# A hybrid decoder layer: merge gates in a stage of their own by seven block products in place of eight, sums moved between VectorE, GpSimd and ScalarE

## The chip, the cores and the metric

The kernel runs on one core of one Trainium2 chip. Five engines take part: TensorE (PE, with its weight loads PEld) multiplies, VectorE (DVE), ScalarE (ACT) and GpSimd (POOL) work on elements, and SyncE (SP) issues most of the DMA transfers; GpSimd issues some. The metric is the device time of one execution in microseconds, the median over runs. A profiled execution gives the trace from which all rows below come.

## What is computed

A decoder layer on 2048 tokens of width 1024, in float32. Of the reference this matters:

```python
h = einsum('bsd,dn->bsn', x, w_in) + b_in      # x: 2048 x 1024
c_q, c_kv, k_pe, z_a, u, v, z_b, g_a, g_b = split_columns(h)
#  384,  128,   32, 512, 512, 512, 512, 1024, 1024 columns
y_a = mla_attention(c_q, c_kv, k_pe, ...) * silu(z_a)   # 8 heads, causal
y_b = spatial_gating(u, v, ...) * silu(z_b)
merged = sigmoid(g_a) * (y_a @ w_oa) + sigmoid(g_b) * (y_b @ w_ob)
out = layer_norm(alpha * x + merged @ w_out)
```

The columns z_a, u, z_b, g_a and g_b are called features here; g_a and g_b are the two merge gates.

## The kernel before

**Precision.** Every float32 factor is cut into a high and a low part. `split` (L65 to L67) does it with a ScalarE cast (high) and a VectorE subtraction (low, L67). `mm3` (L69) then multiplies three times: high by high, high by low, low by high. One such step is three matmuls, nearly always with a 128x128 weight and 512 columns.

**Stages.** x is read in four chunks c of 512 tokens, kept as xh and xl, two chunks at a time. Up to 178.2 us the latents are projected and raised to queries, keys and values. Up to 319.3 the spatial gating unit (SGU) computes v, normalises and mixes it (`mix`), turns the result by `ptu` transposes, and stores it as mo to mxd (L481, L482). Then attention runs with the features as fill, and from 1405.6 on the last stage forms the gated outputs, their product with w_ab, the product with w_out, and the layer norm.

**Features.** There are 28 tiles of 128 columns: ZA, U, ZB with 4 each, GA, GB with 8 each (MT_ORDER is their order). `gates()` is a generator. `weights(m)` loads a tile's weights (fst) and splits them (fwh, fwl, L66 and L67). `group(m, c)` does eight steps into one PSUM tile psg and yields after each. A gate then needs one ScalarE tanh (L525) and a store to gd from GpSimd (L526); the other features pass through `finish` with VectorE operations on ft, fo and gu. Each tile's weights are loaded twice, for chunks 0 and 1 and then for 2 and 3.

**Attention.** Blocks of one head h and one chunk c follow each other, 32 in all. For a block, `top` multiplies queries by keys into pss and VectorE takes row maxima mx (L639); after the last, dg, a diagonal of negated maxima, is built on VectorE (L644) and `shift` turns it into an extra row of Q. `score(k)` multiplies a block of 128 keys, on partitions, by 512 queries (three matmuls into pst); ScalarE takes the exponential p and casts ph, VectorE subtracts pl (L67), and GpSimd adds p to acc (L675). `product` multiplies ph and pl by V into po. Behind the last k, acc is split into ah and al, and `total` sums it over keys. p, ph and pl have three buffers each, pst two in PSUM, Q three.

**Order.** TensorE keeps the order in which the program is written (`keep`). Products lag scores by two steps, tops run up to LEAD = 6 steps ahead by a list of due times. Each call of `work(cost)` adds to a credit, and whenever that reaches half a fill step, one step of `gates()` is put in; `rate` is chosen so that 36 steps are left for the end. 48 steps stand ahead of attention and 12 more near its start. On the other engines a scheduler sets the order; `high_priority` moves work forward.

## Time and profile before

| | us |
|---|---|
| median of three runs (1777.47 to 1780.12) | 1778.77 |
| the profiled execution, its time | 1779.64 |
| the profiled execution, span from first to last instruction | 1777.9 |
| attention with its 48 fills ahead and 36 behind | 319.3 to 1405.6 |

A share is an engine's busy time over the span. A stretch's row tells how long each engine was busy in it and with how many instructions (a few matmul records are missing), and then the clock granted to TensorE as a part of full speed. In a timeline row the bracket tells how long the engine was idle before the instruction and what ended that. Matmuls overlap in the trace, so their rate is read from a stretch and not from one's length.

### The profile page before, as it was taken

What the parts mean: (1) busy time and instruction counts of PE and PEld (TensorE: products, weight loads), DVE (VectorE), ACT (ScalarE), POOL (GpSimd) and SP (SyncE); (2) the same over time, 40 slices, a digit from 0 to 9 for tenths busy, and PEclk for the clock granted to TensorE, in tenths of its full rate; (3) what the DMA queues carried; (4) which work ended last, traced back from release to release, by engine and by line L of the source; (5) the groups of instructions that cost most, each with busy time, mean ns of one, the idle gap of its engine ahead of it and who ended that gap; (6) DMA issues with size and microseconds to landing.
All of it is one profiled execution on the core that took longest, in us unless ns stands there. A gap on an engine that the chain in (4) does not pass through costs nothing.

```text
span 1777.9 us, 23031 instructions
## 1 busy us (share of the span) xinstructions
PE 1712.2 (96%) x8064; PEld 1422.2 (80%) x8064; DVE 1274.9 (72%) x2241; ACT 804.9 (45%) x1468; POOL 471.6 (27%) x520
## 2 busy tenths in 40 slices
PE   8999999999999999999899999899999899999998
PEld 8899877778888778888688887788888678888886
DVE  7855686378877777667788878676766568777664
ACT  6533442245565545456566565455556331303020
POOL 0000011023444334444344444244444000000000
PEclk9999999999999999999899999899999999999999
DMA  6754841721132242142531222421120888667341
GB/s 211 228 194 157 269 158 48 173 94 57 60 113 78 70 140 67 60 128 92 154 111 54 76 83 74 119 84 66 60 77 30 267 281 268 215 197 217 121 130 71
DMA packets 105092, 229.19 MB, mean 129 GB/s; under 512 B 11720, under 2 KB 28360, under 8 KB 103952
## 3 DMA queue, kind: packets, MB, share of 16 engines
q1 hardware_dynamic: 94480, 194.16, 34.8%
q0 software_dynamic: 10496, 33.56, 5.5%
q8 instruction: 63, 1.03, 0.2%
q14 instruction: 53, 0.43, 0.1%
HBM read 155.70 MB, written 71.97 MB: 128 GB/s over the span
## 4 chain that ended last, share of the span: by engine, by line
PE 62%; DVE 7%; ACT 4%; issue 4%; DMA 2%; POOL 0%; SPq 0%; DVEq 0%; ACTq 0%; POOLq 0%
PE psg L87 25%; PE po L87 16%; PE pst L87 9%; PE pb L87 5%; PE pa L87 4%; PE pss L87 3%; DVE pl L67 2%; DVE mx L639 1%; ACT p L669 1%; DMA Q<-qrd 1%; ACT ph L66 1%; DVE fwl L67 1%; DMA wabst<-in_w_ab_dram 1%; PE pbl L87 1%; DVE dg L644 0%
## 5 line engine op out<-in xcount | busy, mean ns | idle before, releaser
L67 DVE TENSOR_TENSOR pl<-p,ph 128x512 fp32r<-128x512 f32 (+1 forms) x320 | 308.9, 966 | 191.7 <-ACT ph L66 182.2
L675 POOL TENSOR_TENSOR acc<-acc,p 128x512 f32<-128x512 f32 (+3 forms) x288 | 333.5, 1158 | 415.9 <-ACT p L669 414.4
L87 PE MATMUL psg<-xh,fwh 128*128 128x512 f32 x896 | 357.9, 399 | 0.0
L87 PE MATMUL psg<-xl,fwh 128*128 128x512 f32 x896 | 355.8, 397 | 0.0
L87 PE MATMUL psg<-xh,fwl 128*128 128x512 f32 x896 | 354.9, 396 | 0.0
L669 ACT ACTIVATE p<-pst 128x512 f32<-128x512 f32 (+1 forms) x320 | 170.7, 534 | 376.4 <-DVE pst L668 174.6
L87 PE MATMUL pst<-Q,K 97*128 97x512 f32 (+3 forms) x960 | 249.4, 368 | 0.0
L87 PEld LDWEIGHTS pst<-Q,K 96*128 96x128 f32 (+1 forms) x960 | 177.0, 192 | 32.9
L639 DVE TENSOR_REDUCE mx<-pss 128x1 f32<-128x512 f32 (+3 forms) x320 | 190.8, 602 | 17.3 <-PE pss L87 13.4
L87 PEld LDWEIGHTS psg<-xh,fwl 128*128 128x128 f32 x896 | 170.9, 191 | 38.1
L87 PEld LDWEIGHTS psg<-xl,fwh 128*128 128x128 f32 x896 | 172.1, 192 | 31.7
L87 PEld LDWEIGHTS psg<-xh,fwh 128*128 128x128 f32 x896 | 171.7, 192 | 31.8
L66 ACT CAST ph<-p 128x512 fp32r<-128x512 f32 (+1 forms) x320 | 178.1, 557 | 9.1
L87 PE MATMUL pss<-K,Q 96*128 96x512 f32 (+2 forms) x320 | 118.1, 382 | 25.5 <-DMA Q<-qrd 17.0
L78 POOL TENSOR_TENSOR rs<-tm,half 128x1 f32<-128x1 f32 x32 | 24.7, 770 | 421.9 <-DVE tm L77 421.9
L87 PE MATMUL po<-ph,V 128*128 128x512 f32 (+1 forms) x320 | 117.0, 366 | 5.4 <-DVE o L694 5.4
L87 PE MATMUL po<-pl,V 128*128 128x512 f32 (+1 forms) x320 | 117.1, 366 | 0.0
L67 DVE TENSOR_TENSOR fwl<-fst,fwh 128x512 fp32r<-128x512 f32 x112 | 88.9, 800 | 23.0 <-ACT fwh L66 22.9
L87 PE MATMUL po<-woh,mh 128*128 128x512 f32 x256 | 100.6, 394 | 0.0
L87 PE MATMUL po<-woh,ml 128*128 128x512 f32 x256 | 99.7, 391 | 0.0
L87 PE MATMUL po<-wol,mh 128*128 128x512 f32 x256 | 99.5, 389 | 0.0
L87 PEld LDWEIGHTS pss<-K,Q 96*128 96x128 f32 x320 | 61.6, 194 | 43.9 <-DVE mx L639 11.0
(219 smaller groups left out, 3092.8 us busy)
## 6 DMA issues: line engine op xcount, KB each, us to landing
fst<-in_w_feat_dram SPq DMA_DIRECT2D x56, 512.0 KB
gd<-fo POOLq DMA_DIRECT2D x96, 256.0 KB, 2.3
wabst<-in_w_ab_dram SPq DMA_DIRECT2D x32, 512.0 KB
xst<-in_xT_dram SPq DMA_DIRECT2D x31, 512.0 KB
kd<-e SPq DMA_DIRECT2D x16, 512.0 KB
vd<-ve SPq DMA_DIRECT2D x16, 512.0 KB
qnd<-e SPq DMA_DIRECT2D x16, 512.0 KB
V<-vd SPq DMA_DIRECT2D x8, 1024.0 KB
```

The source lines that it names most:

```text
L66: act.copy(hi, src)
L67: dve.tensor_tensor(lo, src, hi.bitcast(F32), op=ALU.subtract)
L78: pool.tensor_tensor(dst, tmp, half, op=ALU.pow)
L87: inorder(pe.matmul(*args, **kw))
L639: dve.tensor_reduce(self.mx[:, j, i:i + 1], ps[:, :n], axis=AX.X, op=ALU.max)
L669: act.activation(p[:, q0:], ps[:, q0:], AF.Exp)
L675: pool.tensor_tensor(self.acc[:, q0:], self.acc[:, q0:], p[:, q0:], op=ALU.add)
```

## The change

It has five parts.

1. **Gates.** MT_ORDER loses GA and GB, which leaves 12 feature tiles as fill, 1152 matmuls in place of 2688. A new stage between the SGU and attention computes the gates in 16 quads. A quad is the 2x2 block product of two weight tiles (GA+m, GB+m; their two halves of 512 rows are w11, w21 and w12, w22) with two chunks of x (their halves). It takes seven products (A, B, C, D, E, where A and D take two each) of 4 steps, in place of eight, from sums of blocks (Strassen's method in Winograd's form). Per quad four combinations of weights and seven low parts are GpSimd tensor_tensor operations, seven high parts are ScalarE casts, and VectorE does five additions out of PSUM. Sums of x are made on VectorE once per two chunks, for quads 0 and 8. Results pass through a tanh on ScalarE and a GpSimd store, as before.
2. **fwl** (weights of the remaining features) and **al** go from VectorE to GpSimd.
3. **dg** goes from one VectorE operation to four ScalarE activations of 128x128.
4. **Q** has four buffers, gu two in place of three.
5. The fill takes chunks 2 and 3 first, then 0 and 1, which are loaded again; 45 steps are left for the end. x is kept in halves (`x_half`, `xk`). The last `mix` is put under `high_priority`.

The core of the diff (the sums s3, s2 and s4 are built as s1 is):

```diff
-MT_ORDER = [m for f in range(4) for m in (MT_U + f, MT_ZB + f, MT_ZA + f)] + list(range(MT_GA, MT))
+MT_ORDER = [m for f in range(4) for m in (MT_U + f, MT_ZB + f, MT_ZA + f)]
...
-        mix(*pend)
+        with tc.high_priority():
+            mix(*pend)
+    with ExitStack() as ph:
...
+        def sums(c0, c1, have):
...
+            if not have:
+                halves(a, *xt[c0][0])
+            yield xt[c0][0]
+            if not have:
+                halves(c, *xt[c1][1])
+            yield xt[c1][1]
+            if not have:
+                raw(c0, 1, d)
+                halves(d, *xt[c0][1])
+            yield xt[c0][1]
+            combine(d, b, c, ALU.add)
+            s = new(1)
+            halves(d, *s)
+            yield s
...
+        def columns(m1, m2):
...
+            def cut(v):
+                hi = dw.tile([P, 4, P], F32R, tag="wh", name="dwh")
+                lo = dw.tile([P, 4, P], F32R, tag="wl", name="dwl")
+                act.copy(hi, v)
+                pool.tensor_tensor(lo, v, hi.bitcast(F32), op=ALU.subtract)
+                return hi, lo
+            pool.tensor_tensor(t1, w12, w11, op=ALU.subtract)
+            pool.tensor_tensor(t2, w22, t1, op=ALU.subtract)
+            pool.tensor_tensor(t4, w21, t2, op=ALU.subtract)
+            pool.tensor_tensor(w12, w22, w12, op=ALU.subtract)
+            for v in (w11, t4, w21, t1, w12, t2, w22):
+                yield cut(v)
+        def product(ps, w, x, more=False):
+            for j in range(4):
+                for i, (a, b) in enumerate(((0, 0), (0, 1), (1, 0))):
+                    mm(ps, w[a][:, j, :], x[b][:, j, :], start=not more and j == 0 and i == 0,
...
+        def out_of(src, c, m, add=None):
...
+                dve.tensor_tensor(o, src, add, op=ALU.add)
+                act.activation(o, o, AF.Tanh, scale=0.5, bias=bfh[:, m:m + 1])
+            pool.dma_start(gd[c][m], o)
...
+                if i == 0:
+                    act.copy(self.u2, self.A)
+                elif i == 2:
+                    out_of(self.A, self.c0, self.m1)
+                elif i == 5:
+                    dve.tensor_tensor(self.u2, self.B, self.u2, op=ALU.add)
+                    dve.tensor_tensor(u3, self.C, self.u2, op=ALU.add)
+                    out_of(self.D, self.c1, self.m2, u3)
+                    out_of(self.E, self.c1, self.m1, u3)
+                elif i == 6:
+                    out_of(self.D, self.c0, self.m2, self.u2)
...
+            for i in range(1, NPROD):
+                if i == NPROD - 1 and nx:
+                    nx.run(0)
+                q.run(i)
+                follow()
...
-                split(st[:, k:k + 4, :], wh[:, k:k + 4, :], wl[:, k:k + 4, :])
+                act.copy(wh[:, k:k + 4, :], st[:, k:k + 4, :])
+                pool.tensor_tensor(wl[:, k:k + 4, :], st[:, k:k + 4, :], wh[:, k:k + 4, :].bitcast(F32),
...
-        for cs2 in ((0, 1), (2, 3)):
+        for cs2 in ((2, 3), (0, 1)):
...
-                self.Qt = kp.tile([DH + 1, 2, C], F32R, tag="Q", bufs=3, name="Q")
+                self.Qt = kp.tile([DH + 1, 2, C], F32R, tag="Q", bufs=4, name="Q")
...
-                        dve.tensor_tensor(self.dg, ident.unsqueeze(1).to_broadcast([P, 4, P]),
-                                          nm.to_broadcast([P, 4, P]), op=ALU.mult)
+                        for e in range(4):
+                            act.activation(self.dg[:, e, :], ident, AF.Copy, scale=nm[:, e, :])
...
-                        split(self.acc, self.ah, self.al)
+                        act.copy(self.ah, self.acc)
+                        pool.tensor_tensor(self.al, self.acc, self.ah.bitcast(F32), op=ALU.subtract)
...
-        rate = (len(MT_ORDER) * 4 * 8 - 48 - 12 - 36) * STEP_NS / (cols * MM_NS)
+        rate = (len(MT_ORDER) * 4 * 8 - 48 - 12 - 45) * STEP_NS / (cols * MM_NS)
```

Three places show what is moved. The first is TensorE in the middle of attention; psg is the fill, pst the scores, po the products, pss the tops; a number in a name is that of a buffer. Before, in a row:

```order
L87 MATMUL psg<-xh_8595,fwh 128x512
L87 MATMUL psg<-xl_8596,fwh 128x512
L87 MATMUL psg<-xh_8595,fwl 128x512
L87 MATMUL psg<-xh_8351,fwh 128x512
L87 MATMUL psg<-xl_8352,fwh 128x512
L87 MATMUL psg<-xh_8351,fwl 128x512
L87 MATMUL po<-ph,V 128x512
L87 MATMUL po<-pl,V 128x512
L87 MATMUL psg<-xh_8351,fwh 128x512
L87 MATMUL psg<-xl_8352,fwh 128x512
L87 MATMUL psg<-xh_8351,fwl 128x512
L87 MATMUL pss<-K,Q 128x512
```

and after the change:

```order
L87 MATMUL psg<-x_2950,fwh 128x512
L87 MATMUL psg<-x_2951,fwh 128x512
L87 MATMUL psg<-x_2950,fwl 128x512
L87 MATMUL pst<-Q,K 128x512 x3
L87 MATMUL po<-ph,V 128x512
L87 MATMUL po<-pl,V 128x512
L87 MATMUL pss<-K,Q 128x512
L87 MATMUL psg<-x_2950,fwh 128x512
L87 MATMUL psg<-x_2951,fwh 128x512
L87 MATMUL psg<-x_2950,fwl 128x512
L87 MATMUL pst<-Q,K 128x512 x3
```

A score, its product and a top now follow each other with one step of fill or none between, where two or three stood.

The second is TensorE at the end of the SGU stage. Before, the last transposes and then the first fill:

```order
L479 MATMUL ptu<-ident,um 128x128 [waits Activation_49]
L479 MATMUL ptu<-ident,um 128x128 x3
L87 MATMUL psg<-xh_2948,fwh 128x512
L87 MATMUL psg<-xl_2949,fwh 128x512
L87 MATMUL psg<-xh_2948,fwl 128x512
```

after the change, the same transposes and then the new stage, with what its first matmul waits for (DMASW are the queues of GpSimd's stores):

```order
L477 MATMUL ptu<-ident,um 128x128 [waits Activation_49]
L477 MATMUL ptu<-ident,um 128x128 x3
L87 MATMUL dA<-x_2950,dwh 128x512 [waits DMASW3_49,DMASW4_49,DMASW2_49,DMASW5_49,DMASW1_49,DMASW6_49,DMASW0_49,DMASW7_49,PE_49,Activation_49]
L87 MATMUL dA<-x_2951,dwh 128x512
L87 MATMUL dA<-x_2950,dwl 128x512 [waits Pool_49]
```

The first matmul of the new stage waits for all of GpSimd's stores, where that of the fill waited for none of them.

The third is VectorE behind the SGU stage. Before, features of the first fills (ft, gu, fo) and their weights:

```order
L541 TENSOR_SCALAR ft<-ft 128x512
L542 TENSOR_TENSOR ft<-ft,fo 128x512
L546 SCALAR_TENSOR_TENSOR gu<-ft,fo 128x512
L67 TENSOR_TENSOR fwl<-fst,fwh 128x512 x2
L541 TENSOR_SCALAR ft<-ft 128x512
L542 TENSOR_TENSOR ft<-ft,fo 128x512
L546 SCALAR_TENSOR_TENSOR gu<-ft,fo 128x512
L552 SCALAR_TENSOR_TENSOR fo<-ft,fo 128x512
L554 TENSOR_TENSOR fo<-fo,gu 128x512
L67 TENSOR_TENSOR fwl<-fst,fwh 128x512 x2
```

after the change, between quad 6's last output (do) and quad 7's additions (du, from PSUM tiles dp); x, xsum and s are parts and sums of x for quad 8:

```order
L601 TENSOR_TENSOR do<-dD,du_4551 128x512
L67 TENSOR_TENSOR x_2981<-xraw,x_2980 128x512 x4
L67 TENSOR_TENSOR x_2953<-xsum_3563,x_2952 128x512 x3
L533 TENSOR_TENSOR xsum_3563<-xsum_3562,xraw 128x512 x2
L67 TENSOR_TENSOR x_2953<-xsum_3563,x_2952 128x512
L533 TENSOR_TENSOR xsum_3563<-xsum_3562,xraw 128x512 x2
L67 TENSOR_TENSOR s_4828<-xsum_3563,s_4827 128x512 x4
L533 TENSOR_TENSOR xsum_3562<-xraw,xsum_3562 128x512 x4
L67 TENSOR_TENSOR s_4859<-xsum_3562,s_4858 128x512 x4
L637 TENSOR_TENSOR du_4699<-dp,du_4699 128x512
L533 TENSOR_TENSOR xsum_3563<-xsum_3563,xraw 128x512
L639 TENSOR_TENSOR du_4882<-dp,du_4699 128x512
```

Twenty-four operations on x stand between the two now, in a stage whose outputs go through VectorE.

## Rows read from the trace of the kernel before

**Rows 1.** the page: busy time of each engine, and the stores of features from GpSimd.

```profile
PE 1712.2 (96%) x8064; PEld 1422.2 (80%) x8064; DVE 1274.9 (72%) x2241; ACT 804.9 (45%) x1468; POOL 471.6 (27%) x520
gd<-fo POOLq DMA_DIRECT2D x96, 256.0 KB, 2.3
```

**Rows 2.** stretches from 319.3 on: length, then busy us of each engine (x instructions).

```profile
core 0: us, PE busy (x) PEld busy (x) DVE busy (x) ACT busy (x) POOL busy (x), PEclk, DMA share, GB/s
319.30:352.50 33.20, 33.20 (x146) 27.54 (x145) 9.92 (x17) 10.90 (x18) 3.03 (x6) 0.98 0.87 203
352.50:1378.80 1026.30, 995.40 (x4449) 820.07 (x4447) 773.37 (x1239) 570.84 (x1044) 419.38 (x439) 0.98 0.27 86
1378.80:1405.60 26.80, 26.27 (x117) 21.23 (x115) 13.32 (x21) 9.53 (x16) 2.75 (x5) 1.00 0.79 245
1405.60:1777.90 372.30, 355.43 (x1536) 289.56 (x1536) 259.92 (x394) 76.67 (x98) 15.38 (x17) 0.99 0.59 193
```

**Rows 3.** the same middle stretch, instructions that touch fwl alone.

```profile
352.50:1378.80 1026.30, 322.08 (x812) 154.78 (x811) 82.11 (x102) 0.98 0.27 86
```

**Rows 4.** what TensorE and its weight load waited for, 319.3 to 1405.6: us, times, longest.

```profile
PE pss L87 <- DMA Q<-qrd: 17.0, 5, 4.9
PEld pss L87 <- DVE mx L639: 11.0, 15, 2.6
PEld pss L87 <- DVE al L67: 10.2, 3, 3.4
```

**Rows 5.** short stretches, same columns as Rows 2.

```profile
390.00:400.00 10.00, 10.00 (x45) 8.16 (x44) 9.87 (x17) 6.88 (x12) 5.18 (x5) 1.00 0.27 78
900.00:950.00 50.00, 49.98 (x225) 40.84 (x224) 43.64 (x69) 30.06 (x54) 22.12 (x20) 1.00 0.21 70
1417.00:1423.00 6.00, 6.00 (x14) 4.26 (x15) 3.15 (x5) 1.67 (x2) 0.00 (x0) 0.50 0.95 321
1600.00:1650.00 50.00, 50.00 (x221) 41.30 (x221) 37.41 (x52) 16.98 (x22) 0.00 (x0) 1.00 0.70 217
```

**Rows 6.** VectorE's groups in 352.5 to 1378.8: busy us, mean ns of one.

```profile
L67 DVE TENSOR_TENSOR pl<-p,ph 128x512 fp32r<-128x512 f32 (+1 forms) x320 | 308.9, 966 | 191.7 <-ACT ph L66 182.2 <-PE psg L87 6.8 <-PE pss L87 0.9
L639 DVE TENSOR_REDUCE mx<-pss 128x1 f32<-128x512 f32 (+3 forms) x320 | 190.8, 602 | 17.3 <-PE pss L87 13.4
L67 DVE TENSOR_TENSOR fwl<-fst,fwh 128x512 fp32r<-128x512 f32 x102 | 82.1, 811 | 16.1 <-ACT fwh L66 15.9
L644 DVE TENSOR_TENSOR dg<-ident,nm 128x512 fp32r<-128x512 f32 x32 | 30.6, 956 | 0.7
L67 DVE TENSOR_TENSOR al<-acc,ah 128x512 fp32r<-128x512 f32 x31 | 21.4, 691 | 6.4 <-ACT ah L66 6.0
```

**Rows 7.** GpSimd's groups, shapes kept apart, same columns.

```profile
L675 POOL TENSOR_TENSOR acc<-acc,p 128x512 f32<-128x512 f32 x192 | 260.4, 1356 | 266.8 <-ACT p L669 265.5
L526 POOL DMA_DIRECT2D gd<-fo x64 | 36.2, 565 | 74.7 <-ACT fo L525 70.5 <-issue 3.6
```

**Rows 8.** timeline (start, length in us): acc and pl together, and pl alone.

```profile
611.50 0.69 DVE L67 TENSOR_TENSOR pl<-p,ph 128x512 fp32r<-128x512 f32 x1 [1.31 <-ACT ph L66]
...
728.96 1.29 POOL L675 TENSOR_TENSOR acc<-acc,p 128x512 f32<-128x512 f32 x1 [1.05 <-ACT p L669]
729.49 1.31 DVE L67 TENSOR_TENSOR pl<-p,ph 128x512 fp32r<-128x512 f32 x1 [1.30 <-ACT ph L66]
```

**Rows 9.** timeline at the end of the SGU stage, and behind the last fill.

```profile
319.42 0.78 PE L87 MATMUL psg<-xh,fwh 128*128 128x512 f32 x1
324.64 0.17 DVE L591 MEMSET maskt<- 128x128 f32 x1 [7.95 <-DMA mxd<-mo]
...
1416.87 0.80 PE L87 MATMUL pb<-ybh,wabh 128*128 128x512 f32 x1 [4.79 <-ACT wabh L66]
```

**Rows 10.** ScalarE's groups in 319.3 to 1405.6.

```profile
L66 ACT CAST fwh<-fst 128x512 fp32r<-128x512 f32 x108 | 66.1, 614 | 20.9 <-PE psg L87 20.3
L525 ACT ACTIVATE fo<-psg,bfh 128x512 f32<-128x512 f32 x63 | 43.2, 685 | 10.1 <-PE psg L87 6.8 <-issue 2.8
```

More of the change, by code (lines that the diff above doesn't have):

```diff
@@ L126, in hybrid_layer_kernel, with x_half, xk, x_pieces @@
     xt = {}
-    def x_pieces(c):
-        hi = xp.tile([P, KD, C], F32R, tag="xh", name=f"xh{c}")
-        lo = xp.tile([P, KD, C], F32R, tag="xl", name=f"xl{c}")
-        xt[c] = (hi, lo)
-        for k in range(0, KD, 2):
+    def x_half(c, f):
+        xt.setdefault(c, {})[f] = tuple(xp.tile([P, 4, C], F32R, tag=f"x{f}{e}", name=f"x{f}{e}{c}") for e in range(2))
+    def xk(c, k):
+        return tuple(x[:, k % 4, :] for x in xt[c][k // 4])
+    def x_pieces(c, halves=(0, 1)):
+        for f in halves:
+            x_half(c, f)
+        for k in range(4 * halves[0], 4 * halves[-1] + 4, 2):
             st = xs.tile([P, 2, C], F32, tag="st", name="xst")
@@ L136, in x_pieces @@
                 yield
-                split(st[:, j, :], hi[:, k + j, :], lo[:, k + j, :])
+                split(st[:, j, :], *xk(c, k + j))
     def load_x(c):
@@ L156, in hybrid_layer_kernel @@
     wll = wl_.tile([P, KD, LAT], F32R, name="wll")
-    hi0 = xp.tile([P, KD, C], F32R, tag="xh", name="xh0")
-    lo0 = xp.tile([P, KD, C], F32R, tag="xl", name="xl0")
+    x_half(0, 0)
+    x_half(0, 1)
     for k in range(0, KD, 2):
@@ L166, in hybrid_layer_kernel @@
         for j in range(2):
-            split(st[:, j, :], hi0[:, k + j, :], lo0[:, k + j, :])
+            split(st[:, j, :], *xk(0, k + j))
             split(ws[:, j, :], wlh[:, k + j, :], wll[:, k + j, :])
-    xt[0] = (hi0, lo0)
     blat = wl_.tile([P, LAT], F32, name="blat")
@@ L252, in latent @@
     def latent(c, ts):
-        xh, xl = xt[c]
         pss = {}
@@ L264, in latent @@
             cs = slice(h2 * 272, (h2 + 1) * 272)
-            mm3(pss[t, h2], (xh[:, k, tk], xl[:, k, tk]),
+            mm3(pss[t, h2], tuple(x[:, tk] for x in xk(c, k)),
                 (wlh[:, k, cs], wll[:, k, cs]), k == 0, k == KD - 1)
@@ L382, in gelu_v @@
         def gelu_v(c, t):
-            xh, xl = xt[c]
             tk = slice(t * P, (t + 1) * P)
@@ L387, in gelu_v @@
             for k in range(KD):
-                mm3(ps, (xh[:, k, tk], xl[:, k, tk]), (wvh[:, k, :], wvl[:, k, :]),
+                mm3(ps, tuple(x[:, tk] for x in xk(c, k)), (wvh[:, k, :], wvl[:, k, :]),
                     k == 0, k == KD - 1)
@@ L411, in hybrid_layer_kernel @@
         uctx.close()
-        fw_cm = tc.tile_pool(name="fw", bufs=2, side="right")
-        fw = fw_cm.__enter__()
-        psg_cm = tc.tile_pool(name="p3G", bufs=2, space=PSUM, side="right")
-        ps_g = psg_cm.__enter__()
         wp = ph.enter_context(tc.tile_pool(name="p2w", bufs=1))
@@ L500, in gates @@
+    fw_cm = tc.tile_pool(name="fw", bufs=2, side="right")
+    fw = fw_cm.__enter__()
+    psg_cm = tc.tile_pool(name="p3G", bufs=2, space=PSUM, side="right")
+    ps_g = psg_cm.__enter__()
     def gates():
@@ L508, in weights @@
             for k in range(0, KD, 4):
-                split(st[:, k:k + 4, :], wh[:, k:k + 4, :], wl[:, k:k + 4, :])
+                act.copy(wh[:, k:k + 4, :], st[:, k:k + 4, :])
+                pool.tensor_tensor(wl[:, k:k + 4, :], st[:, k:k + 4, :], wh[:, k:k + 4, :].bitcast(F32),
+                                   op=ALU.subtract)
             return wh, wl
@@ L514, in group @@
         def group(m, c, wh, wl):
-            xh, xl = xt[c]
             ps = ps_g.tile([P, C], F32, tag="g", name="psg")
             for k in range(KD):
-                mm3(ps, (wh[:, k, :], wl[:, k, :]), (xh[:, k, :], xl[:, k, :]),
+                mm3(ps, (wh[:, k, :], wl[:, k, :]), xk(c, k),
                     k == 0, k == KD - 1)
@@ L544, in finish @@
                 yield
-                g = fw.tile([P, C], F32, tag="gu", bufs=3, name="gu")
+                g = fw.tile([P, C], F32, tag="gu", bufs=2, name="gu")
                 dve.scalar_tensor_tensor(g, t, 1.0, o, op0=ALU.add, op1=ALU.mult)
@@ L555, in finish @@
                 pool.dma_start(gd[c][m], o)
-        for cs2 in ((0, 1), (2, 3)):
+        for cs2 in ((2, 3), (0, 1)):
             ms_ = [[m] for m in MT_ORDER]
-            ms_ = (ms_[:-2] + [ms_[-2] + ms_[-1]] if cs2[0] == 0 else
+            ms_ = (ms_[:-2] + [ms_[-2] + ms_[-1]] if cs2[0] == 2 else
                    [ms_[0] + ms_[1]] + ms_[2:])
@@ L564, in gates @@
                 for c in cs2:
-                    pieces = (x_pieces(2) if c == 1 and ms is ms_[-1] else
-                              x_pieces(3) if c == 2 and ms is ms_[0] else iter(()))
+                    pieces = (x_pieces(0) if c == 3 and ms is ms_[-1] else
+                              x_pieces(1) if c == 0 and ms is ms_[0] else iter(()))
                     for m in ms:
```

103 lines of the change are left out of this document (98 added, 5 removed).

## The prediction, made before the change was run

> **What bounds the kernel now.** I read the busy shares first, then the stretches, then the waits. TensorE works 96% of the span and VectorE 72% [rows 1], so over the whole program TensorE is the limit. By stretches [rows 2] this holds in attention too, but with less room: from 352.5 to 1378.8 TensorE is busy 995 of 1026 us and VectorE 773. That is the stretch to look into, because 812 of its 4449 matmul records belong to the low-weight third of a feature step [rows 3], so 812 steps of three matmuls, some 2436 matmuls, are fill: they have nothing to do with attention and keep TensorE busy while softmax runs on the other engines. Take them away and TensorE's own attention work is far below 773 us. What TensorE waits for there now is small: 17.0 us on Q loads, 21 us of weight loads behind VectorE [rows 4]. Where VectorE is densest it is 9.87 of 10 us busy with TensorE still full [rows 5]; over a longer stretch 43.6 of 50.
>
> The unit price is that of a 128x512 matmul at the full clock, 2.4 GHz: 50 us / 221 = 0.226 us [rows 5]. At the half clock, 14 matmuls took 6.0 us right behind a wait of 4.79 us [rows 5, 9]. So a wait of some 5 us costs itself and about 6.0 - 14 x 0.226 = 2.8, say 3 us more.
>
> **The new stage.** It begins where the first fill began, at 319.3 [rows 2]. Sixteen quads of seven products of 12 matmuls are 1344 matmuls, x 0.226 = **303.7 us**; they replace 16 x 4 x 8 x 3 = 1536, so the saving in matmuls is 192 x 0.226 = 43.4 us, the whole gain of the change. Against it stand:
> - Entry. The order shows the stage's first matmul and its weight cuts waiting for the last stores of mxd, whose memory the new tiles take. In the trace they land at 324.64, while TensorE could go on at 319.42 [rows 9]. With one cast of 0.61 us [rows 10] that is 324.64 + 0.61 - 319.42 = **5.8 us**, and 3 at the half clock.
> - Sums of x. VectorE makes 32 two-input operations for quad 0, of which 24 stand behind the same wait, and 44 for quad 8. One costs 0.69 us alone, and 1.31 beside a GpSimd sum [rows 8]. At quad 0 the 24 take 17 to 31 us against 22 us until the last of them is needed (seven earlier products of 2.7 us and the half clock): 0 to 9 us late. For quad 8 the order puts 24 such operations into VectorE's row between quad 6's last output and quad 7's additions. From that output on 30 operations (the 24, another sum, the output, quad 7's two additions and two outputs), 21 to 39 us, must be done before TensorE may write the last product of quad 7, which comes 16.3 us (six products) later: 4 to 23 us late. GpSimd is nearly always running in this stage (below), which speaks for the dear end; its own pauses while TensorE waits speak against it. I take 4 + 11, and 2.5 for the last product, which has no next quad to hide VectorE's three operations: **18 us** (7 to 35).
> - GpSimd. A quad asks 11 sums (four combinations of weights, seven cuts) at some 1.29 us [rows 8] and four stores' issues at 0.565 [rows 7]: 16.5 us, under TensorE's 84 x 0.226 = 19.0. Hidden, but by 2.5 us only. The seven ScalarE casts, 7 x 0.61, and VectorE's five additions have room.
> - Exit. Attention's first fill has the stage's last stores to wait for: an addition (0.69), a tanh 0.685, an issue 0.565, a landing 2.3 and a cast 0.61 [rows 1, 6, 7, 10] are **4.9 us**, and 3 at the half clock.
>
> Sum: 5.8 + 3 + 303.7 + 18 + 4.9 + 3 = **338.4 us**. Neither the 48 fills ahead (33.2 us [rows 2], now of the first feature tiles) nor the last stage (372.3) is changed in kind; the latter's first loads now want chunk 0's last features, whose store (0.565 to issue, 2.3 to land) has chunk 1's last eight steps, 5.4 us, to hide in. The fills behind attention grow from 36 to 45: 26.8 + 9 x 3 x 0.226 = 32.9. All but attention's core, T, is then 319.3 + 338.4 + 33.2 + 32.9 + 372.3 = 1096.1 us. Against the span of 1777.9 **the change pays if T is under 682 us**.
>
> **Attention's core, T.** Of the 812 fills 291 stay (12 x 4 x 8 = 384, less 48 and 45); 521 x 3 x 0.226 = 353 us leave TensorE.
> - TensorE's bound: 1026.3 - 353 = 673; if the fourth Q buffer takes away the 17.0 us of Q waits, **656**.
> - VectorE's bound. Moved off it are fwl 82.1, dg 30.6 and al 21.4: 773.4 - 134.1 = 639.3 us. The other feature groups' work stays whole, since the gates had almost nothing on VectorE. But the length of its operations isn't fixed. pl alone took 0.69 us; started while acc ran on GpSimd it took 1.31 and ended just behind it [rows 8]. The mean of its 320, 0.966 [rows 6], lies between. GpSimd had 419 us of work in the core [rows 2]; it now loses the gates' issues (about 57 x 0.565 = 32) and gains 38 cuts of fwl (48 less the ten that fell outside the core before) and 31 of al, 69 x 1.29 = 89: 476 us, in a shorter stretch, so 68% of it instead of 41%. I charge each of the 69 one meeting with a two-input operation of VectorE: 69 x (1.31 - 0.69) = 43. VectorE: **682 us**. The ends: all pl at 0.69, 320 x (0.966 - 0.69) = 88 less than 639, is 551; all of them at 1.31, 110 more than 639, is 749.
> - How full can VectorE get? 9.87 of 10 us at its densest, 43.6 of 50 over a longer stretch [rows 5], there with TensorE as the limit. Here TensorE, 656 of the same time, has few spare fills to hide a wait with, so I don't take the densest row: 97%, and stay nearer to it than to the 87% because products may lag two steps and tops run six steps ahead. **T = 682 / 0.97 = 703 us.**
>
> dg is now four ScalarE activations of 128x128 instead of one VectorE operation. ScalarE had 571 us [rows 2]; it loses some 64 casts (39 us) and 57 gate tanh (39 us) and gains 128 short activations, so it ends near 530 of 703: not the bound. The added wait is exp's on GpSimd (a p buffer is free when acc has read it): a late acc, queued behind two fwl cuts of 1.29 us, holds exp and all that stands behind it on ScalarE, and then the scores, which have two PSUM buffers.
>
> The move of fwl and al is where the notes speak against the change. The row: pl beside acc took 1.31 us in place of 0.69, and acc takes 1.29, or 1.36 in the mean [rows 7, 8]. The Trainium skill ("GPSIMD Engine Reference", sections 1 and 4.1) says that GpSimd shares its SBUF interfaces with VectorE and contends with VectorE instructions that have two SBUF inputs, and that GpSimd is about half as fast at two-input elementwise work. The trace agrees with both. If the moved work were free, VectorE's 639 us would give 659 and the kernel would be faster; with what the page says, less is moved than appears.
>
> **The sum.** 1096.1 + 703 = 1799; the profiled run is 1779.64 for a span of 1777.9, so 1.7 lie outside: **1801 us**. That run stands 0.9 above the median of 1778.77; I don't correct for it. The change is +1.2% on it. A difference under 0.2% (3.6 us) is within what a measurement of this kernel can tell from none.
>
> **Rivals.**
> 1. TensorE stays the bound in attention (faster). pl's price falls, since the cuts on GpSimd come when VectorE works on PSUM (mx) or on one input; VectorE is then at 640 or below and T is 656 to 675. The time is 1096 + 665 + 2 = **1763** (1754 to 1773). For it: pl's mean already holds 0.276 of the possible 0.62 us; the fourth Q buffer. Against: 656 and 640 side by side leave no slack. Chance 0.28.
> 2. The loop of attention becomes bound by latency (slower still). Exp, cast, pl and acc of one score wait for each other, VectorE only reaches the 87% of the longer stretch, and TensorE falls to 1.2 GHz between. T = 682 / 0.873 = 781, the time **1879**. It decides if a step's chain no longer fits into two steps, 2 x 703/320 = 4.4 us; cast and pl are 0.61 + 1.31, and with exp taken like the cast 2.5 us in a free row, so it needs queues as well. For it: fewer fills. Chance 0.14.
> 3. GpSimd bounds the new stage (slower). It does if a sum takes over (19.0 - 2.3) / 11 = 1.52 us; each 0.1 us more is 17.6 us in sixteen quads. At 1.6 us about 15 us: **1816**. Against: acc keeps its 1.29 beside VectorE. Chance 0.08.
> 4. T is at the break-even, the stage's stalls near their cheap end: within 0.2%, 1775 to 1782. Chance 0.08.
>
> My forecast, VectorE bound by shared ports with T from 685 to 740, gets 0.42 (1783 to 1840). Slower: 0.42 + 0.14 + 0.08 = 0.64, cut to 0.63 and the rest to rival 1: faster 0.29, same 0.08. The range for 8 in 10 leaves out the dearest part of rival 2 and the cheapest of rival 1: 1755 to 1855.
>
> **What would show it.** Right: the new stage is 330 to 350 us, with two gaps on TensorE at quads 0 and 7, each behind x sums; in the core VectorE is over 93% busy, TensorE under 95%, pl's mean is over 1.05 us, and TensorE's waits name pl and mx. Wrong: TensorE at 97% in the core with pl under 0.95 us (rival 1); VectorE under 90% with a granted clock under 0.93 in the core (rival 2); the new stage over 360 us with GpSimd without pauses in every quad (rival 3). What would undo the forecast most simply is T under 682 us.

## The result, and the profile after

The changed kernel takes 1896.06 us (median of four runs, 1890.41 to 1901.11) against 1779.44 before: slower, ratio 1.0653, 95% interval 1.0619 to 1.0688. The profiled execution took 1890.41 us with a span of 1888.7. I had said 1801, slower, with a range up to 1855: the direction was right, the size was not.

The page of the changed kernel, its first part, and then its stretches with the columns of [rows 2] (new stage, fills ahead, attention's core, fills behind, last stage):

```profile
PE 1715.2 (91%) x7872; PEld 1393.2 (74%) x7872; DVE 1295.8 (69%) x2225; ACT 898.5 (48%) x1708; POOL 835.4 (44%) x776
```

```profile
319.30:689.50 370.20, 323.82 (x1361) 260.33 (x1361) 135.51 (x165) 145.65 (x246) 269.06 (x241) 0.93 0.37 120
689.50:724.50 35.00, 34.86 (x146) 28.27 (x146) 8.74 (x11) 11.38 (x20) 11.74 (x11) 0.95 0.97 222
724.50:1484.40 759.90, 668.58 (x2883) 526.78 (x2883) 653.27 (x1062) 515.27 (x1035) 496.79 (x445) 0.97 0.23 68
1484.40:1517.40 33.00, 32.46 (x144) 26.64 (x143) 18.01 (x26) 14.42 (x23) 6.19 (x6) 0.99 0.69 229
1517.40:1888.70 371.30, 356.40 (x1537) 289.12 (x1535) 262.03 (x399) 77.73 (x101) 15.76 (x18) 0.99 0.58 190
```

Against [rows 2] the sum closes: the new stage adds 370.2, the core loses 1026.3 - 759.9 = 266.4, the fills add 1.8 and 6.2, the last stage loses 1.0: +110.8 us, which is 1888.7 - 1777.9. Taken out of the core were 353 us of matmuls, and it became only 266 shorter. Of the missing 87, 60 are idle time of TensorE (31 us before, 91 now), the rest lies in its busy time, which fell by 327 and not by 353. In the core TensorE is busy 88% and VectorE 86%: neither is full.

What TensorE waited for in the whole span (us, times, longest), the rows that matter, first those of the new stage:

```profile
PE dD L87 <- DVE do L601: 22.7, 5, 14.8
PE psg L87 <- ACT fwh L689: 9.5, 1, 9.5
PE dA L87 <- ACT dwh L578: 8.7, 1, 8.7
PE dA L87 <- ACT du L633: 3.1, 1, 3.1
PE dp L87 <- DVE s L67: 1.2, 2, 0.7
...
PE po L87 <- DVE pl L67: 46.2, 44, 5.1
PE pbm L87 <- ACT dg L820: 13.2, 8, 4.6
PE po L87 <- DVE o L870: 12.2, 13, 2.3
PE pss L87 <- DVE mx L814: 11.9, 17, 2.5
```

[rows 4] had 17.0 us of Q waits; no row names Q now. In its place stand results of VectorE, pl 46.2, o 12.2 and mx 11.9, and ScalarE's dg, 13.2, which is made from VectorE's maxima. VectorE's row for pl in the core, to be held against [rows 6]:

```profile
L67 DVE TENSOR_TENSOR pl<-p,ph 128x512 fp32r<-128x512 f32 (+1 forms) x320 | 317.1, 997 | 63.7 <-ACT ph L66 60.1 <-PE pss L87 1.8
```

Its mean mixes four widths. For the 224 of 512 columns alone, before and then after:

```profile
L67 DVE TENSOR_TENSOR pl<-p,ph 128x512 fp32r<-128x512 f32 x224 | 247.1, 1103 | 140.1 <-ACT ph L66 130.9 <-PE psg L87 6.8 <-PE pss L87 0.9
L67 DVE TENSOR_TENSOR pl<-p,ph 128x512 fp32r<-128x512 f32 x224 | 255.1, 1142 | 55.0 <-ACT ph L66 52.0 <-PE pss L87 1.8
```

A quiet step of a long block, from the timeline (start, length, engine, operation, idle time before it; weight loads, a cast and TensorE's six other matmuls are left out):

```profile
990.16 1.30 POOL L850 TENSOR_TENSOR acc<-acc,p 128x512 f32<-128x512 f32 x1 [1.48 <-ACT p L844]
...
990.55 0.87 PE L87 MATMUL pst<-Q,K 97*128 97x512 f32 x3
990.71 1.31 DVE L67 TENSOR_TENSOR pl<-p,ph 128x512 fp32r<-128x512 f32 x1 [0.99 <-ACT ph L66]
...
991.51 0.60 ACT L844 ACTIVATE p<-pst 128x512 f32<-128x512 f32 x1 [0.84 <-POOL acc L850]
...
991.93 0.68 DVE L814 TENSOR_REDUCE mx<-pss 128x1 f32<-128x512 f32 x1
...
992.64 0.87 PE L87 MATMUL pst<-Q,K 97*128 97x512 f32 x3
```

One step lasts 992.64 - 990.55 = 2.09 us, nine matmuls without a pause. VectorE needs pl and mx, 1.31 + 0.68 = 1.99 us of it, because pl runs beside acc. So in such a step TensorE is the limit, and VectorE has 0.1 us to spare. That whatever a feature or a block's end adds to VectorE is then waited for is a reading of this step; the waits above fit it.

### The profile page after: what moved, and what is told of

Same layout as the page of the kernel before. It is cut to its first block, busy times and chain, and to the rows that moved or that the text cites. A ratio compares the mean times of both kernels' runs of the same rounds, so it can differ in the third digit from the quotient of the medians.

```text
span 1888.7 us, 23439 instructions
## 1 busy us (share of the span) xinstructions
PE 1715.2 (91%) x7872; PEld 1393.2 (74%) x7872; DVE 1295.8 (69%) x2225; ACT 898.5 (48%) x1708; POOL 835.4 (44%) x776
## 4 chain that ended last, share of the span: by engine, by line
PE 55%; DVE 22%; ACT 8%; issue 6%; DMA 5%; POOL 4%; SPq 0%; ACTq 0%; POOLq 0%; DVEq 0%
PE po L87 12%; DVE pl L67 7%; PE psg L87 6%; PE dp L87 6%; PE dD L87 4%; PE pa L87 4%; PE pb L87 4%; PE dA L87 4%; PE pst L87 4%; DVE mx L814 3%; PE psl L87 3%; PE psa L87 3%; ACT p L844 2%; POOL acc L850 2%; ACT ph L66 2%
## 5 line engine op out<-in xcount | busy, mean ns | idle before, releaser
L850 POOL TENSOR_TENSOR acc<-acc,p 128x512 f32<-128x512 f32 (+3 forms) x288 | 347.4, 1206 | 200.1 <-ACT p L844 181.2
L87 PE MATMUL psg<-x,fwh 128*128 128x512 f32 x768 | 246.8, 403 | 9.5 <-ACT fwh L689 9.5
L814 DVE TENSOR_REDUCE mx<-pss 128x1 f32<-128x512 f32 (+2 forms) x320 | 189.7, 601 | 17.7 <-PE pss L87 15.3
L87 PEld LDWEIGHTS psg<-x,fwh 128*128 128x128 f32 x768 | 147.6, 195 | 37.8 <-ACT fwh L689 10.0
L87 PE MATMUL po<-pl,V 128*128 128x512 f32 (+1 forms) x320 | 125.3, 392 | 46.8 <-DVE pl L67 46.2
L87 PE MATMUL psg<-x,fwl 128*128 128x512 f32 x384 | 153.9, 401 | 0.1
L87 PE MATMUL po<-ph,V 128*128 128x512 f32 (+1 forms) x320 | 121.6, 380 | 14.4 <-DVE o L870 12.2
L87 PE MATMUL pss<-K,Q 96*128 96x512 f32 (+2 forms) x320 | 119.6, 387 | 13.0 <-DVE mx L814 11.9
L637 DVE TENSOR_TENSOR du<-dp,du 128x512 f32<-128x512 f32 x16 | 11.0, 690 | 162.5 <-PE dp L87 149.1
L87 PEld LDWEIGHTS po<-pl,V 128*128 128x128 f32 x320 | 62.1, 194 | 76.0 <-DVE pl L67 65.5
L87 PE MATMUL psl<-wlh,x 128*128 128x272 f32 x512 | 102.0, 294 | 6.2 <-ACT wlh L66 6.2
L87 PE MATMUL dD<-s,dwh 128*128 128x512 f32 x256 | 84.3, 412 | 22.7 <-DVE do L601 22.7
L66 ACT CAST wabh<-wabst 128x1024 fp32r<-128x1024 f32 x32 | 33.7, 1052 | 146.1 <-PE pa L87 124.6
```

The source lines that it names most:

```text
L66: act.copy(hi, src)
L87: inorder(pe.matmul(*args, **kw))
L637: dve.tensor_tensor(self.u2, self.B, self.u2, op=ALU.add)
L814: dve.tensor_reduce(self.mx[:, j, i:i + 1], ps[:, :n], axis=AX.X, op=ALU.max)
L850: pool.tensor_tensor(self.acc[:, q0:], self.acc[:, q0:], p[:, q0:], op=ALU.add)
```

## The experiments

The theories, as the expectations name them. P: GpSimd's sums lengthen VectorE's two-input operations (the shared port), so that work moved to GpSimd frees nothing. W: VectorE simply has too much work, wherever GpSimd stands. M: the moved operations queue in front of the softmax on GpSimd or ScalarE. L: latency, two steps of lag and three buffers are too few without fill.

In each table row below the core is the stretch from the first top to the last sum over keys, which is 762.1 us for the changed kernel and 1026.8 before. The four executions of the changed kernel differ by up to 11 us, and the profiled one is the fastest of them. Most of this scatter lies in the core: e10, e11 and e12 below have the same attention, and their cores take 757.6, 773.3 and 772.3 us. So a difference of the core under some 15 us says nothing by itself; there the times of several executions decide. e3, e4 and e12 were executed once.

**Which of the moves costs (e1, e2).** The changed kernel with fwl and al back on VectorE:

```diff
-                act.copy(wh[:, k:k + 4, :], st[:, k:k + 4, :])
-                pool.tensor_tensor(wl[:, k:k + 4, :], st[:, k:k + 4, :], wh[:, k:k + 4, :].bitcast(F32),
-                                   op=ALU.subtract)
+                split(st[:, k:k + 4, :], wh[:, k:k + 4, :], wl[:, k:k + 4, :])
-                        act.copy(self.ah, self.acc)
-                        pool.tensor_tensor(self.al, self.acc, self.ah.bitcast(F32), op=ALU.subtract)
+                        split(self.acc, self.ah, self.al)
```

> The low parts of the feature weights (fwl) and of the row sums (al) are taken back from GpSimd to VectorE; all else is the changed kernel, whose attention core took 759.9 us (VectorE 653 busy, GpSimd 497). Theory P (shared port: what is moved to GpSimd slows VectorE by about as much as it takes off it): VectorE busy rises by less than 25 us, GpSimd falls by some 95, the core stays at 745 to 775 and the time at 1880 to 1910. Theory W (plain work: VectorE has too much of it, wherever GpSimd stands): VectorE busy +50, the core 800 to 820, time 1940 to 1955. Theory M (the moved operations queue in front of the softmax sums on GpSimd and hold the loop): core 700 to 725, time 1835 to 1860.

and with dg back:

```diff
-                        for e in range(4):
-                            act.activation(self.dg[:, e, :], ident, AF.Copy, scale=nm[:, e, :])
+                        dve.tensor_tensor(self.dg, ident.unsqueeze(1).to_broadcast([P, 4, P]),
+                                          nm.to_broadcast([P, 4, P]), op=ALU.mult)
```

> The diagonal dg goes back from four ScalarE activations to one VectorE operation; all else is the changed kernel. Theory P or W (VectorE is the limit): VectorE +31 us, core 780 to 800, time 1910 to 1935. Theory M (ScalarE's row holds dg up; 13 us of waits of TensorE and 17 of weight loads on it): core 740 to 750, time 1875 to 1890.

| | time | core | VectorE busy | GpSimd busy | pl, ns |
|---|---|---|---|---|---|
| changed | 1896.1 | 762.1 | 653.5 | 498.3 | 997 |
| e1, fwl and al back | 1877.6 | 752.1 | 661.5 | 397.1 | 891 |
| e2, dg back | 1902.6 | 772.1 | 676.2 | 502.7 | 985 |

e1: VectorE took back 70 operations, 63.1 us of work (fwl 39.8, al 23.3), and is busy only 8 us more, since pl fell from 997 to 891 ns. That is theory P's sign. The time is 18 us better (1875 to 1884 against 1890 to 1901), just under P's 1880: here the move did not merely free nothing, it cost 18 us. e2: with dg back the median is 6.5 us worse, but the executions overlap (1898 to 1904), and the time lies between the two ranges expected. That moving dg helps is seen more clearly in e14 below.

**VectorE's operations beside GpSimd's (e3, e4, e9, e15).** Without the additions to acc, so that the row sums are not formed (the 1.0 is added to what stands in their place):

```diff
-                    else:
-                        pool.tensor_tensor(self.acc[:, q0:], self.acc[:, q0:], p[:, q0:], op=ALU.add)
...
-                    dve.tensor_scalar(l1, l1, 2.0, None, op0=ALU.mult)
+                    dve.tensor_scalar(l1, l1, 2.0, 1.0, op0=ALU.mult, op1=ALU.add)
```

> GpSimd's additions of the exponentials to acc are left out (only the first key block is copied), so the row sums are not formed; GpSimd loses 347 us of 497 in the core. Theory P: pl falls from a mean of 1.0 to 0.7 us or less, VectorE to 540 to 570 us, the core to 665 to 690 and the time to 1795 to 1820. Theory W: pl and the core hardly move, 740 or more. Theory L (latency: products lag by only two steps and three buffers, so each chain of exponential, cast and low part is waited for): pl's own 0.3 us less takes some 30 us off, core 715 to 740.

and without pl (the high part is multiplied twice in its place):

```diff
-                    split(p[:, q0:], hi[:, q0:], lo[:, q0:])
+                    act.copy(hi[:, q0:], p[:, q0:])
-                self.p[k] = hi, lo, q0
+                self.p[k] = hi, hi, q0
```

> The low part pl is left out and the high part is multiplied twice, so TensorE's work is the same and VectorE loses 317 us. It shows what TensorE's own bound in the core is: 656 us by the matmuls. Theories P, W and L all expect 655 to 680 us and a time of 1785 to 1810; if the core stays above 700, neither VectorE nor the chain through pl is what holds it, but dg, the tops or the Q loads.

The same work with pl reading p from PSUM, which takes away one of its two SBUF inputs, and then that with fwl and al back:

```diff
-                p = pp.tile([P, C], F32, tag="p", name="p")
+                p = ps
-                        pool.tensor_copy(self.acc, p)
+                        pool.tensor_copy(self.acc, hi.bitcast(F32))
-                        pool.tensor_tensor(self.acc[:, q0:], self.acc[:, q0:], p[:, q0:], op=ALU.add)
+                        pool.tensor_tensor(self.acc[:, q0:], self.acc[:, q0:], hi[:, q0:].bitcast(F32), op=ALU.add)
```

> The changed kernel, but the exponential is written back in place to PSUM, so that pl's subtraction reads one input from PSUM and one from SBUF; GpSimd adds up the high parts alone (the low parts are left out of the row sums). The work of every engine and the number of instructions stay. Theory P (two SBUF inputs against GpSimd's sums): pl's mean falls from 1.0 to 0.75 us or less though GpSimd works as before, VectorE to 560 to 590 us, the core from 762 to 680 to 720, the time to 1810 to 1850. Theory W: pl and the core stay. If PSUM is held too long (two score buffers, now kept until pl and acc have read them), TensorE's waits move to pst and the core stays above 730.

> The changed kernel with both cures: p kept in PSUM (GpSimd sums the high parts alone) and fwl and al back on VectorE. Theory P: no more contention than acc's own, the core from 713 to 685 to 710, time 1815 to 1840. Theory W (VectorE's load counts): fwl and al add 50 us to VectorE, the core 725 or more, time 1850 or more.

VectorE's rows for pl in the core of e3, and of e9:

```profile
L67 DVE TENSOR_TENSOR pl<-p,ph 128x512 fp32r<-128x512 f32 (+1 forms) x320 | 225.2, 708 | 66.8 <-ACT ph L66 64.6
```

```profile
L67 DVE TENSOR_TENSOR pl<-pst,ph 128x512 fp32r<-128x512 f32 (+1 forms) x320 | 192.6, 605 | 101.9 <-ACT ph L66 99.8
```

| | time | core | VectorE busy | GpSimd busy |
|---|---|---|---|---|
| changed | 1896.1 | 762.1 | 653.5 | 498.3 |
| e3, no additions to acc | 1796.9 | 668.7 | 534.7 | 146.7 |
| e4, no pl | 1801.5 | 669.9 | 373.4 | 466.2 |
| e9, p in PSUM | 1842.5 | 713.2 | 522.6 | 463.4 |
| e15, p in PSUM, fwl and al back | 1828.4 | 700.5 | 551.0 | 373.7 |

e4 shows what TensorE can reach: 670 us, of which it is busy 641. e3 reaches the same with VectorE doing all its operations, only because GpSimd's additions are gone: pl falls to 708 ns. e9 keeps GpSimd busy (463 us) and still has pl at 605, so it is the two SBUF inputs beside GpSimd that lengthen it; 49 us of the core go. Most of what e9 keeps above 670 is a new wait of TensorE, its first row now:

```profile
PE pst L87 <- DVE pl L67: 37.1, 47, 3.2
```

The score buffers in PSUM are held until pl has read them, as the expectation feared in part. In e15 VectorE has 28 us more to do than in e9 and the kernel is 14 us faster: the load of VectorE by itself, theory W, is not what counts there. It must be added that e3 and e9 also change when a buffer of p is free again, so they don't price the port alone.

Theory M would show on ScalarE, where the exponential waits until GpSimd's acc has read a buffer of p. ScalarE's row for that (us, times, longest), in the core of the changed kernel and then of e4:

```profile
ACT p L844 <- POOL acc L850: 31.5, 34, 2.5
ACT p L843 <- POOL acc L849: 31.9, 46, 1.0
```

In e4 the exponential waits as long for acc as in the changed kernel, and the core is at 670: this wait alone does not hold the loop. In e1, with fwl and al off GpSimd, it is still 28.1 us, so the moved operations add little to it. The core falls to TensorE's limit when either GpSimd's additions (e3) or VectorE's pl (e4) go. So it is the two side by side that make it slow. e4 also takes 280 us of work off VectorE, and e3 and e9 change when p is free: that pl's greater length alone is the cause, and not also the buffers of p, is likely by this but not shown.

**The lag (e7, e8).**

Three Q buffers again (bufs=4 to bufs=3 at the tile Q):

> The changed kernel with three Q buffers again; the control for the next one. In the changed kernel no wait on Q loads is left. All theories: the core 765 to 785 us, time 1895 to 1915, with Q waits of 10 to 25 us back.

and with them a longer lag:

```diff
-                later(2)
+                later(3)
                 ahead(step)
-                if len(todo) > 2:
-                    later(2)
+                if len(todo) > 3:
+                    later(3)
-                hi = pp.tile([P, C], F32R, tag="ph", name="ph")
-                lo = pp.tile([P, C], F32R, tag="pl", name="pl")
+                hi = pp.tile([P, C], F32R, tag="ph", bufs=4, name="ph")
+                lo = pp.tile([P, C], F32R, tag="pl", bufs=4, name="pl")
```

> As the one before (three Q buffers), but products lag scores by three steps in place of two, and ph and pl have four buffers. Theory L: the waits of products on pl (46 us, 65 of weight loads) go, the core is 40 to 60 us shorter than with three Q buffers alone, 710 to 730. Theories P and W: a longer lag only evens out bursts, 0 to 20 us shorter.

With three Q buffers the core is 793.2 us (1922.3 in time), more than the 785 (1915) expected: the fourth is worth 31 us there, 26 in time, and 20.2 us of Q waits are back. With products lagging three steps it is 774.2 (1906.2): 19 us less, 16 in time, at the upper end of what P and W allow. TensorE's waits in its core:

```profile
PE po L87 <- DVE o L870: 25.1, 17, 3.3
PE pbm L87 <- ACT dg L820: 23.1, 12, 4.1
PE pss L87 <- DMA Q<-qrd: 22.5, 6, 6.3
PE pss L87 <- DVE mx L814: 18.3, 25, 3.1
PE pst L87 <- ACT p L844: 9.2, 16, 1.2
PE po L87 <- DVE pl L67: 3.5, 6, 1.7
```

The wait on pl went from 46.9 to 3.5 us and came back at o, dg and mx, the other things VectorE makes or feeds. TensorE is idle 105.5 us of the core in e7 and 103.3 in e8; nearly all of the 19 us lies in its busy time (687.7 and 670.9). So the short lag tells where the waiting shows, not how much there is.

**The new stage (e10, e11, e12).** Eight plain products in a stage of their own, made with the fill's code in place of the quads:

```diff
+    keep[0] = True
+    for _ in gates(list(range(MT_GA, MT)), ((0, 1), (2, 3)), True):
+        pass
+    keep[0] = False
+    fill = gates(MT_ORDER, ((2, 3), (0, 1)), False)
```

> The stage for the gates stays apart, but computes eight plain products with the fill's own code (1536 matmuls, no sums of x or weights, no additions out of PSUM); attention is that of the changed kernel. If the seven products save their 44 us less only small stalls, the stage is about 348 to 355 us against the present 370 from the end of the SGU stage to the first fill, since the entry (13.5), the x sums of quads 0 and 8 (about 25) and the exit (9.5) go with it: 1865 to 1880 us. If the stalls belong to any stage that stands there, the stage is 375 or more, 1895 to 1910.

The sums of x made once (made holds quad 0's):

```diff
+            if not have:
+                yield
+                yield xt[c0][0]
+                yield xt[c1][1]
+                yield xt[c0][1]
+                for n in (1, 3, 2, 4):
+                    yield made[n]
+                return
             a, c = raw(c0, 0), raw(c1, 1)
```

> The sums of x are made for quad 0 alone and used for both halves (the second half's x is left out). The stall at quad 7 was 14.9 us, with half-clock matmuls behind. If VectorE's 24 operations in front of quad 7's outputs are its cause, the gap goes, the stage is 15 to 18 us shorter and the time 1873 to 1881; if GpSimd's cuts cause it, it stays.

Keys, values and queries loaded later:

```diff
+        for _ in range(16):
+            next(fill)
         hds = {0: head(0)}
...
-        for _ in range(48):
+        for _ in range(32):
```

> Keys, values and queries of the first blocks are loaded 16 fill steps later. In the changed kernel the last store of the gate stage landed 6.4 us after its issue, where the median is 2.7, with all DMA engines busy on these loads, and TensorE waited 9.5 us for it. If the loads lengthen the landing, the wait falls to 5 to 6 us; if the store is slow by itself, it stays at 9 or more.

e10 takes 1871.2 us: **eight products are 25 us faster than seven** in this place. In the trace its 1680 matmuls of gates and first fills follow one another from 323.3 to 704.8, and TensorE is busy in all of these 381.5 us; the changed kernel reaches that point, the first top, 19.5 us later at 724.3. The rest is mostly the core (757.6), within its scatter. The saved 43.4 us were more than eaten by entry, sums and exit, and by the half clock behind their waits (a granted clock of 0.93 in the stage, 1.00 in e10 up to 704.8). In e11 the 14.85 us gap at quad 7 is gone, and from the first product to the last it is 330.6 us in place of 346.7, 16 less: VectorE's sums of x in front of quad 7's outputs were its cause. The time expected, 1873 to 1881, was missed: it fell only to 1886.1, with a core of 773.3 in the profiled execution. e12 shows nothing: the loads were issued at the same point behind the last product as before (0.45 us after it), in spite of the later place in the program, and the wait stayed at 9.5.

What held the entry and the exit, from the timeline: the last store of each, and the first cast behind it; then the DMA share (last but one column) of the stretch ahead of the exit's end:

```profile
326.60 0.54 POOL L480 DMA_DIRECT2D mxd<-mo  x1 [0.34 <-ACT mo L479]
...
332.23 0.62 ACT L578 CAST dwh<-dst 128x512 fp32r<-128x512 f32 x1 [5.92 <-DMA mxd<-mo]
...
681.86 0.58 POOL L603 DMA_DIRECT2D gd<-do  x1 [0.48 <-ACT do L602]
...
688.82 0.62 ACT L689 CAST fwh<-fst 128x512 fp32r<-128x512 f32 x1 [7.25 <-DMA gd<-do]
```

```profile
682.50:689.00 6.50, 0.00 (x0) 0.00 (x0) 0.00 (x0) 0.18 (x1) 0.00 (x0) 0.54 1.00 257
```

The last store of the stage was issued by 682.44 and landed at 688.8, 6.4 us after. Counted from the start of the issue, as [rows 1] does with its 2.3, it is 6.8, and the median of this stage's 64 stores is 2.7. All that time the DMA engines were 100% busy with the keys, values and queries that SyncE had begun to load at 680. That the loads delay the store is likely by that, but not shown: e12 was to show it and did not move them.

**The moves and the fourth Q buffer on the kernel before (e5, e6, e13, e14, e16, e17).** Here TensorE is the limit, with all its fill. The edits are those above, made in the kernel before, and for Q:

```diff
-                self.Qt = kp.tile([DH + 1, 2, C], F32R, tag="Q", bufs=3, name="Q")
+                self.Qt = kp.tile([DH + 1, 2, C], F32R, tag="Q", bufs=4, name="Q")
-                g = fw.tile([P, C], F32, tag="gu", bufs=3, name="gu")
+                g = fw.tile([P, C], F32, tag="gu", bufs=2, name="gu")
```

> The kernel before, with its 812 fills in the core, and only the three moves: fwl and al to GpSimd, dg to ScalarE. TensorE is the limit there (97% of the core), so theories P and W expect no change (1772 to 1786) since VectorE has room either way; theory M, by which the moved operations hold the loop, expects it slower by 15 us or more. A gain of over 5 us would say that VectorE's bursts cost TensorE something even with full fill.

> The kernel before with a fourth Q buffer (and two of gu in place of three) and nothing else. Its TensorE waits 17.0 us for Q loads in attention, with half-clock matmuls behind. If these waits go, 1750 to 1762 us; if the Q loads are late for another reason (the tops wait for something else next), 1770 to 1780.

> The kernel before with four Q buffers (1757.2 us) and fwl alone moved to GpSimd. If the move of fwl is what cost 31 us in the run of all three moves, 1775 to 1790; if it is al or dg, 1754 to 1762.

> The kernel before with four Q buffers (1757.2 us) and dg alone moved to four ScalarE activations. VectorE loses 31 us of one thousand: if tops and outputs wait for VectorE's bursts there (9.8 and 5.5 us), 1748 to 1757; if ScalarE's row delays dg as it did in the changed kernel (13 us of waits), 1758 to 1770.

> The kernel before with four Q buffers and p kept in PSUM (GpSimd sums the high parts alone). TensorE is its limit, so a VectorE with less work gains at most the waits on mx and o that are left (some 17 us with the half clock): 1742 to 1757; if PSUM's score buffers are held too long, as in the changed kernel (37 us of waits on pst), 1760 to 1790.

> The kernel before with four Q buffers, p kept in PSUM (GpSimd sums the high parts alone) and dg on ScalarE. The two last gave 7 and 12 us over four Q buffers alone. If they take away the same waits (VectorE's bursts at small blocks), 1741 to 1747; if different ones, 1733 to 1740; if dg's four activations stand in front of the exponentials once VectorE has room, 1748 or more.

| kernel before with | time | ratio to before (95%) | core |
|---|---|---|---|
| all three moves (e5) | 1810.6 | 1.0165 (1.0147 to 1.0183) | 1053.6 |
| Q in four buffers (e6) | 1757.2 | 0.9871 (0.9855 to 0.9888) | 1003.1 |
| four Q, fwl moved (e13) | 1782.8 | 1.0013 (1.0000 to 1.0026) | 1026.6 |
| four Q, dg moved (e14) | 1749.9 | 0.9831 (0.9808 to 0.9854) | left out: the profiled execution, 1740.7, is 9 under the other four |
| four Q, p in PSUM (e16) | 1744.9 | 0.9800 (0.9780 to 0.9819) | 992.0 |
| four Q, p in PSUM, dg moved (e17) | 1740.4 | 0.9790 (0.9773 to 0.9806) | 987.0 |

e5 contradicts what I had P and W expect: a kernel bound by TensorE lost 31 us to moves that I thought it could not feel. It came out as theory M had it. e13 finds the one that costs most: fwl on GpSimd takes 25.5 us over e6. The cores of e6 and then of e13, in the columns of [rows 2], and e13's pl:

```profile
353.50:1356.60 1003.10, 983.56 (x4449) 809.81 (x4447) 769.88 (x1240) 570.06 (x1045) 415.32 (x439) 1.00 0.28 87
```

```profile
356.20:1382.80 1026.60, 992.19 (x4449) 813.11 (x4447) 768.33 (x1138) 569.05 (x1045) 563.27 (x541) 0.99 0.27 85
```

```profile
L67 DVE TENSOR_TENSOR pl<-p,ph 128x512 fp32r<-128x512 f32 (+1 forms) x320 | 360.0, 1127 | 204.4 <-ACT ph L66 198.1 <-PE psg L87 5.5
```

VectorE has 102 operations less (x1240, x1138), 80.2 us of work in e6, and is as busy as ever, 768.3 against 769.9; pl went from 966 to 1127 ns. GpSimd took 148 us on. The move gave VectorE nothing. TensorE's waits on mx rose from 9.8 to 17.0 us and on o from 5.5 to 12.1, while the exponential's wait for acc, M's sign, rose only from 10.1 to 13.9. So P's mechanism fits here too; wrong was my expectation that a VectorE with room hides it.

e6 beats both kernels with two numbers changed (Q in four buffers, gu in two), e17 the kernel before by 2.1% with three edits. e14 and e16 lie 7 and 12 us under e6, as expected if TensorE waits for VectorE's bursts; e17 gains only 4.5 more on e16, so they mostly take away the same waits. e16 and e17 sum the high parts of the exponentials alone in the row sums, the low parts are left out there.

## Why the prediction was wrong

- **Attention's core: the step that failed** is T = VectorE's work / 0.97, that is, VectorE as the full engine of the core. I put it at 682 us of work and 97% full, T = 703. It had 653 us and was 86% full, T = 760; 653 / 0.97 would have been 673. I had two rows for the share, 98.7% and 87.3% [rows 5], and took the dense one, with TensorE full beside it. TensorE has none to spare at 656 of 700, and with bursts of work on VectorE neither engine then stays full: that is my reading, and no run shows it by itself. What the runs show is that VectorE's work does not set T: in e15 it has 28 us more than in e9 and the core is 13 us shorter, and the core falls to 669 us, with VectorE 80% busy, when GpSimd's additions beside it go (e3). Of the signs I named, TensorE under 95% and the waits on pl and mx came; VectorE over 93% and pl over 1.05 us did not.
- **VectorE's work** missed by 29 us the other way. The charge of 43 us for meetings with GpSimd was not too high: e1 prices the same moves at 55, since 63.1 us of operations went off VectorE and it is busy only 8 less. Too high was the base: without fwl, dg and al VectorE has 598 us in e1, not 639, and 26 of these 41 are pl, at 891 ns instead of 966. The ends of 551 and 749, and the 0.276 of 0.62 us in rival 1, are wrong as well: they put the price of 512 columns on all 320 pl, of which 96 are narrower. The 224 of 512 columns took 1.103 us already before.
- **The direction was in part luck.** The whole miss is 90 us, 57 in the core and 32 in the new stage. With VectorE's measured 653 us, the share of 97% and the stage as said, the sum would have been 1096 + 673 + 2 = 1771, faster than before.
- **TensorE's bound, rival 1's floor,** was right: 656 to 675 said, 669 and 670 in e3 and e4. The rival itself fell, because pl did not get cheaper (997 ns after, 966 before).
- **Rival 2** has the number (VectorE at 87%, 1879) but not its mechanism: the core's granted clock is 0.97, not under 0.93, and a longer lag gives 19 us. Its chance, 0.14, was too small, and the range to 1855 left it out.
- **The new stage,** 338.4 said, 370.2 measured:

| | said | trace after |
|---|---|---|
| entry, to the first product | 5.8 | 332.9 - 319.3 = 13.6 |
| 16 quads | 303.7 | 16 x 19.25 = 308.0 |
| waits inside (VectorE's do 22.7 and s 1.2, ScalarE's du 3.1) | 18 | 27.0 |
| exit, 680.0 to 689.5 | 4.9 | 9.5 |
| half clock and the rest (what is left of 370.2) | 6 | 12.1 |

The places are the ones named: 7.8 us (s 1.2, du 3.1, do 3.5) around quad 0 against 4 said, and 14.85 at quad 7 against 11 said, by e11 shown to be the sums. GpSimd had room there too: 9.9 of the 15.1 us of quad 7's gap, with VectorE busy in all of them. Of the entry, 8.7 us are the wait for the stores; the last transpose of the SGU stage itself starts at 323.7 in place of 319.3, and e10, which has no sums, has it at 323.2 too. Why that part ends later stays open. What I had taken from the wrong row is the landing of stores. From the end of its issue, the last store of the SGU stage took 2.0 us before (issued by 322.7, landed at 324.64) and 5.1 now (issued by 327.1, landed at 332.2), and the last of the new stage 6.4, both beside loads that this stage brings with it. That the loads are the reason is not shown (e12).
- **GpSimd as the stage's bound (rival 3)** did not come. A quad without sums of x, in the columns of [rows 2], keeps TensorE busy throughout, with GpSimd at 16.6 of 19.25 us:

```profile
402.70:421.95 19.25, 19.25 (x86) 15.77 (x85) 3.36 (x5) 7.36 (x13) 16.62 (x17) 1.00 0.34 110
```

- **The last stage and the fills** came as said: 371.3 against 372.3, 33.0 against 32.9, 35.0 against 33.2.
- **The sentence on the Trainium skill** ("GPSIMD Engine Reference", section 1: shared interfaces, contention with instructions of two SBUF inputs) is borne out by these runs. e13 shows the balance of such a move: 80 us off VectorE, 79 back. e9 shows the other half: with one input in PSUM the same subtraction runs in 605 ns, with GpSimd as busy as before (65% of the core).

Of the 110.8 us of loss in the two profiles, 92 are the core above e4's 670 and 20 the stage above e10's. By this estimate the change without either would have come out where the kernel before stands, and e6, the kernel before with its fourth Q buffer, is still 22 us below that.

## What to carry to other kernels

Fill that has nothing to do with the loop costs less inside it than its own time: out of a loop in which a second engine is 75% busy, 353 us of matmuls were taken, and together with the moves that gave only 266 us. Before work is moved from VectorE to GpSimd, count the operations with two SBUF inputs that run beside it: with 320 of them, the move gave back 8 of 63 us here (e1) and 2 of 80 in the kernel before (e13). One input from PSUM (49 us of the core in e9) or a move to ScalarE (7 us in e14) gave more. And a saved product must be set against the entry, the sums and the exit of the stage that makes it possible; here they cost more than one product in eight.
